# A state-space mixer: input tables from factors transposed once, tables by three products and two sums, stores from ScalarE's queue

## The chip, the cores and the metric

The kernel runs on one core of one Trainium2 chip. The metric is the device time of one execution, in microseconds (us); the figure given for a kernel is the median over its runs. The core has TensorE for matmuls and transposes (PE; its weight loads are shown apart as PEld), VectorE (DVE), ScalarE (ACT), GpSimd (POOL) and SyncE (SP), which here does nothing but issue transfers. A queue of transfers is served in the order in which its engine issues them, and an issue that waits for something holds back all that stand behind it.

## The reference

The program is a trunk of two layers on an input x of 1 x 1024 x 1024 in float32. Layer 0 projects the normalised input once, to an input u of a state-space mixer, to the queries, keys and values of a retention mixer, and to two gates; the two results are gated, put side by side and projected back. Layer 1 is a convolution module. The change touches only the state-space mixer of layer 0, which has 64 groups of 16 channels and 64 complex states each:

```python
    dt = jnp.exp(log_dt.astype(f32))[:, None]
    mag = jnp.exp(are * dt)
    lb_re = mag * jnp.cos(aim * dt)
    lb_im = mag * jnp.sin(aim * dt)
...
    bb_re = coef_re[..., None] * bre - coef_im[..., None] * bim
    bb_im = coef_re[..., None] * bim + coef_im[..., None] * bre
...
        bu_re = jnp.einsum('tbgh,gnh->tbgn', u_c, bb_re)
        bu_im = jnp.einsum('tbgh,gnh->tbgn', u_c, bb_im)
        pr, pim, zr, zi = lax.associative_scan(
            _complex_affine_combine, (a_r, a_i, bu_re, bu_im), axis=0)
        xr = zr + pr * s_re - pim * s_im
        xi = zi + pr * s_im + pim * s_re
        y = (jnp.einsum('tbgn,ghn->tbgh', xr, cre)
             - jnp.einsum('tbgn,ghn->tbgh', xi, cim)
             + dsk * u_c)
```

## The kernel before

**Stages.** The large products of layer 0's front are 128-column blocks of the input projection: u0 to u7, then the gates as blocks 8 to 23, then keys and values. Each block is two halves of 512 tokens, and each half is 8 x 3 matmuls of 128x512 (`mm3`, L276 to L278): operands are split into a high and a low part, and high by high, high by low and low by high are summed. u leaves for `u_d` in DRAM, the gates for `gs_d` and `gr_d`.

**The state-space part** runs beside the gates, one block of 8 groups (B = 0 to 7) for every two gate blocks. 1024 tokens are cut into 128 pieces of 8. For each B:

- `s5_tables(B)`: GpSimd makes three pairs of tables as outer products, through `outer`, six instructions a pair: Mr and Mi (powers of lambda 0 to 7 times the input coefficients bb; L790 to L792), the rotations Tc and Ts, and the output table W3 (powers 1 to 8 times C). ScalarE makes R8. These 18 instructions follow each other in a fixed chain over all blocks.
- `s5_states(B)`: U is loaded (L830). TensorE transposes Mr and Mi, four 128x128 pieces each (`w2r`, `w2i`, L837), ScalarE copies them to W2 (L839), and `v` = W2 by U (L848, 16 products). VectorE rotates, scans and rotates back on the bank of `v`, which gives the states S (L856 and following). Then `kp` (L882, L883; 8 products): the response within a piece of 8 tokens, from block-diagonal tables of C (`s_s_cbr`, `s_s_cbi`, loaded ready-made, 1 MB together) by Mr and Mi. ScalarE copies it to Kg (L885), VectorE adds the skip term `dd` to 16 columns, TensorE transposes it (`kt`, L888), ScalarE copies it to Kt (L890), it is stored to `k_d` (L892), and loaded back in Toeplitz form as Wd (L895), which ScalarE reorders into W1 (L897).
- `s5_out(B-1)`: `y` (24 products, L912 and L918) from W1 by U and W3 by S; ScalarE copies it to yb, which is stored to `y_d`.

Beside this the gate stage carries side work of other stages, each with its loads and stores: sums of the input, and on VectorE sums of the output projection's weights (`weight_sums`, `a` and `ws`).

**Before the first block**, `s5_params` makes the coefficients on VectorE, in a long chain of small instructions beside the u blocks; its last ones, bbr and bbi (L607, out of `s5bb`), are GpSimd's. Then the first tables follow (L785 to L792).

**What sets the order.** A scheduler places the instructions of each engine by a simulated timeline, within data dependences, numbers of buffers, `chained` (one instruction after another of its engine) and `issue_after` (not placed ahead of the named instruction). All transfers of this part are issued from SP's queue, as are all weight loads (`wf`). Pools `sums` and `s5w` open when the pool `ev` of the early tiles closes.

Of the kernel before, what the change touches and what calls it, by code (L numbers as in the profile page):

```python
# [57 lines left out]
class Trunk:  # L58
# [278 lines left out]
    def layer0_front(self, st):  # L337
# [100 lines left out]
        def u_block(nb):  # L438
            ut = uv.tile([P, 8, P], F32, name=f"ut_{nb}", tag="ut", bufs=2)

            def evac(h, ps):
# [3 lines left out]
                    r.rearrange("p (m j) -> p j m", j=8), op=ALU.mult)  # L445
            if nb < 2:
                for h in range(2):
                    evac(h, u01[nb][h])
# [4 lines left out]
        def gate_block(nb, w, dst):
# [8 lines left out]
            nc.sync.dma_start(dst[k * P:(k + 1) * P], gt[:])  # L462
# [18 lines left out]
        for nb in range(8, 24):
            B = (nb - 8) // 2
            if nb % 2 == 0:
                self.s5_states(B)
# [101 lines left out]
    def s5_params(self, sp, tp):  # L586
# [35 lines left out]
        v.tensor_scalar(self.cbni[:], self.cbni[:], -1.0, None, op0=ALU.mult)  # L622
# [162 lines left out]
    def outer(self, B, o_r, o_i, ar, ai, br, bi, view, op_r=ALU.subtract, op_i=ALU.add):  # L785

        gp = self.nc.gpsimd
        for o, op, (a0, b0), (a1, b1) in ((o_r, op_r, (ar, br), (ai, bi)), (o_i, op_i, (ar, bi), (ai, br))):
# [1 line left out]
            yield gp.tensor_tensor(view(t[:]), a1, b1, op=ALU.mult)  # L790
            yield gp.tensor_tensor(view(o), a0, b0, op=ALU.mult)
            yield gp.tensor_tensor(o, o, t[:], op=op)  # L792

    def s5_tables(self, B):
# [977 lines left out]
```

## Time and profile before

| | |
|---|---|
| median of 3 runs | 1176.35 us (1176.0 to 1176.86) |
| profiled execution: span | 1173.9 us, 2.45 under the median |
| TensorE busy (PE) | 1161.3 us, 99% |
| VectorE busy | 910.5 us, 78% |
| ScalarE busy | 545.1 us, 46% |
| GpSimd busy | 713.5 us, 61% |
| DMA | 270.66 MB, mean 231 GB/s |

The profile is of one execution. Its span runs from the first to the last instruction, and the medians hold something more around it. Busy time is the time in which an instruction runs on an engine, without waits, branches and transfer issues. A row of a group gives the line, the engine, the operation, the outputs and inputs by the program's names, shapes and the count; a row of a timeline begins with the start, in us from the span's start, and the duration. A matmul's duration is from its start to its modelled end, and overlaps with the next one's, so prices of TensorE's work are taken from distances between starts. The state-space blocks stand between about 100 and 345 us of the span.

### The profile page before, as it was taken

The numbers are of one execution on the slowest core, as the hardware profiler recorded it, in microseconds if no ns is written. First come the engines' busy times: TensorE is split into PE (matmuls) and PEld (weight loads), VectorE is DVE, ScalarE is ACT, GpSimd is POOL, SyncE is SP. The second block draws the span as 40 slices with busy tenths as digits, with TensorE's granted clock in tenths as the row PEclk, the third lists the DMA queues.
The fourth block names the chain that finished last, engine by engine and source line by source line (L and its number), as shares of the span: only waits on it lengthen the run. The fifth ranks groups of instructions, "written<-read, shape, count | busy, mean of one in ns | idle before, by whom it ended". The sixth has DMA issues, their size and how long they took to land.

```text
span 1173.9 us, 17492 instructions
## 1 busy us (share of the span) xinstructions
PE 1161.3 (99%) x6150; PEld 965.5 (82%) x6150; DVE 910.5 (78%) x1507; ACT 545.1 (46%) x821; POOL 713.5 (61%) x507
## 2 busy tenths in 40 slices
PE   9999999999999999999999999999999999999997
PEld 7888888888888888887788888888888888888887
DVE  7875789999717475689777888479999999999643
ACT  7212343332226642123645544367756678544662
POOL 2049999888843245664444034348894689977742
PEclk9999999999999999999999999999999999999999
DMA  9353378778789765765988468965448553357863
GB/s 344 109 178 109 134 270 312 272 269 282 273 307 325 268 228 192 251 190 180 362 313 304 160 220 268 309 232 188 161 158 306 216 182 132 134 176 243 281 247 138
DMA packets 131192, 270.66 MB, mean 231 GB/s; under 512 B 12832, under 2 KB 41760, under 8 KB 130976
## 3 DMA queue, kind: packets, MB, share of 16 engines
q1 hardware_dynamic: 129952, 265.35, 66.5%
q10 hardware_dynamic: 1152, 4.19, 0.9%
q8 instruction: 48, 0.79, 0.3%
q14 instruction: 40, 0.33, 0.1%
HBM read 193.54 MB, written 71.76 MB: 226 GB/s over the span
## 4 chain that ended last, share of the span: by engine, by line
PE 91%; DMA 4%; DVE 2%; SPq 1%; ACT 1%; POOL 1%; issue 1%; DVEq 0%; POOLq 0%; ACTq 0%
PE mm_g L277 8%; PE mm_g L278 8%; PE mm_g L276 7%; PE mm_w L278 4%; PE mm_w L277 4%; PE mm_w L276 4%; PE mm_a L278 2%; PE mm_b L277 2%; PE mm_a L276 2%; PE mm_b L278 2%; PE mm_a L277 2%; PE mm_b L276 2%; PE mm_u L278 2%; PE mm_oc L278 2%; PE mm_u L277 2%; PE mm_oc L277 2%
## 5 line engine op out<-in xcount | busy, mean ns | idle before, releaser
L1461 DVE SCALAR_TENSOR_TENSOR cv<-u,convw,cv 128x512 f32<-128x512 f32 x358 | 244.7, 750 | 5.0 <-ACT cv L1447 3.5
L1441 POOL TENSOR_TENSOR tp<-tp,tp 128x512 f32<-128x512 f32 x104 | 138.9, 1338 | 28.7 <-ACT tp L1440 23.4
L278 PE MATMUL mm_g<-xh,wl_g 128*128 128x512 f32 x256 | 100.8, 394 | 0.0
L277 PE MATMUL mm_g<-xl,wh_g 128*128 128x512 f32 x256 | 100.7, 394 | 0.0
L276 PE MATMUL mm_g<-xh,wh_g 128*128 128x512 f32 x256 | 100.5, 393 | 0.0
L1440 ACT ACTIVATE tp<-u,convw 128x512 f32<-128x512 f32 x104 | 69.6, 713 | 9.6 <-POOL tp L1441 9.4
L277 PEld LDWEIGHTS mm_g<-xl,wh_g 128*128 128x128 f32 x256 | 48.1, 188 | 11.2 <-issue 1.6
L278 PEld LDWEIGHTS mm_g<-xh,wl_g 128*128 128x128 f32 x256 | 48.0, 188 | 10.5
L276 PEld LDWEIGHTS mm_g<-xh,wh_g 128*128 128x128 f32 x256 | 48.1, 188 | 9.6
L278 PE MATMUL mm_oc<-zh,wl_woc 128*128 128x512 f32 (+1 forms) x152 | 54.5, 360 | 0.2 <-DMA wl_woc<-lo_woc 0.2
L276 PE MATMUL mm_oc<-zh,wh_woc 128*128 128x512 f32 (+1 forms) x152 | 54.3, 362 | 0.0
L277 PE MATMUL mm_oc<-zl,wh_woc 128*128 128x512 f32 (+1 forms) x152 | 54.0, 357 | 0.0
L276 PE MATMUL mm_glu<-yh,wh_glu 128*128 128x512 f32 x128 | 50.0, 392 | 1.3 <-ACT sg L1250 1.3
L277 PE MATMUL mm_u<-xl,wh_u 128*128 128x512 f32 x128 | 50.1, 391 | 1.0 <-DVE xl L390 0.9
L276 PE MATMUL mm_g<-h1h,wh_cg 128*128 128x512 f32 x128 | 50.3, 393 | 0.0
L276 PE MATMUL mm_a<-h1h,wh_ca 128*128 128x512 f32 x128 | 50.3, 393 | 0.0
L278 PE MATMUL mm_b<-h1h,wl_cb 128*128 128x512 f32 x128 | 50.3, 393 | 0.0
L232 ACT CAST lh<-lf 128x512 fp32r<-128x512 f32 x32 | 19.5, 618 | 65.9 <-DMA lf<-w_c 59.3
L278 PE MATMUL mm_a<-h1h,wl_ca 128*128 128x512 f32 x128 | 50.0, 391 | 0.0
L277 PE MATMUL mm_glu<-yl,wh_glu 128*128 128x512 f32 x128 | 50.0, 392 | 0.0
L278 PE MATMUL mm_g<-h1h,wl_cg 128*128 128x512 f32 x128 | 49.9, 390 | 0.0
L277 PE MATMUL mm_g<-h1l,wh_cg 128*128 128x512 f32 x128 | 49.9, 390 | 0.0
(811 smaller groups left out, 3637.3 us busy)
## 6 DMA issues: line engine op xcount, KB each, us to landing
wf_g<-w_ab SPq DMA_DIRECT2D x16, 512.0 KB, 5.4
a<-w_out SPq DMA_DIRECT2D x32, 256.0 KB, 4.4
ws<-a SPq DMA_DIRECT2D x32, 256.0 KB, 4.8
lf<-w_c SPq DMA_DIRECT2D x32, 256.0 KB, 5.3
wf_p<-ws SPq DMA_DIRECT2D x16, 512.0 KB, 4.1
wf_cb<-w_c SPq DMA_DIRECT2D x16, 512.0 KB, 4.9
wf_ca<-w_c SPq DMA_DIRECT2D x16, 512.0 KB, 4.7
wl_cb<-lo_cb SPq DMA_DIRECT2D x16, 512.0 KB, 3.4
```

The lines of the kernel that those rows point to most:

```text
L232: self.nc.scalar.copy(hi[:], f[:])
L276: nc.tensor.matmul(ps, wh[:, kb, :], xh, start=start, stop=False)
L277: nc.tensor.matmul(ps, wh[:, kb, :], xl, start=False, stop=False)
L278: self.last_mm = nc.tensor.matmul(ps, wl[:, kb, :], xh, start=False, stop=stop)
L1440: nc.scalar.mul(sk[:], u[:, k:k + HALF], cw[:, nb, k:k + 1])
L1441: gp.tensor_tensor(s0[:], s0[:], sk[:], op=ALU.add)
L1461: v.scalar_tensor_tensor(dst[:], *tap, accs_[i][:], op0=ALU.mult, op1=ALU.add)
```

## The change

Five things are done.

1. *Input tables from transposed factors.* After the first half of u6, `s5_turned` transposes the powers of lambda and bb once (12 transposes in three groups, three copies, four stores to DRAM). For each block four transposed factors are loaded, 256 KB each, repeated over partitions (PT and BT), and GpSimd multiplies them to W2 directly, six instructions without broadcast views. The transposes w2 and their copies go. U's load moves from `s5_states` into `s5_tables`.
2. *Three products and two sums.* Tc, Ts and W3 are made by `outer3`, five instructions a pair, from sums and differences of the factors that are made once.
3. *kp from the output table.* W3 grows to nine powers, and kp is a block-diagonal table of bb (filled by ScalarE) by W3. The skip term is added by four products of 16 columns with slices of the identity. kp comes out the other way round, so kt, its copy and VectorE's addition go, and Kg is stored in eight parts, with runs of 64 bytes.
4. *Queues.* The stores of the gates, of y and of k go from ScalarE's queue.
5. *Pools.* `ev` stays open through u6; the tiles of two temporary pools get fewer buffers. `input_sums_made` follows the last state instruction in place of the addition to Kg.

```diff
@@ layer0_front
             def evac(h, ps):
...
+                if (nb, h) == (6, 0):
+                    with tc.issue_after(self.last_mm.ins):
+                        self.s5_turned(ev)
...
-            nc.sync.dma_start(dst[k * P:(k + 1) * P], gt[:])
+            nc.scalar.dma_start(dst[k * P:(k + 1) * P], gt[:])
...
         u_block(4)
+        for nb in (5, 6):
+            u_block(nb)
         early.close()
         sums = self.pool("sums", 1, stack=st)
         self.s5 = self.pool("s5w", 1, stack=st)
-        for nb in range(5, 8):
-            u_block(nb)
+        u_block(7)
...
-                    with self.tc.issue_after(self.last_kg.ins):
+                    with self.tc.issue_after(self.last_s.ins):
                         self.input_sums_made(*odd)
@@ s5_params
-        self.cbr, self.cbni = load("s5_cbr", (NP, 32)), load("s5_cbi", (NP, 32))
+        self.bblk = [sp.tile([P, NP, 32], F32, name=f"s5_bblk{c}") for c in "ri"]
+        for b in self.bblk:
+            nc.gpsimd.memset(b[:], 0.0)
...
-        v.tensor_scalar(self.cbni[:], self.cbni[:], -1.0, None, op0=ALU.mult)
...
+        tt(self.psum[:], pr_[:], pi_[:], ALU.add)
...
+        tt(self.e2s[:], e2r[:], e2i[:], ALU.add)
+        tt(self.e1s[:], e1r[:], e1i[:], ALU.add)
+        self.last_phase = tt(e1i[:], e1i[:], e1r[:], ALU.subtract)
...
+        tt(self.cdif[:], self.cr[:], self.nci[:], ALU.add, gp)
+        tt(self.csum[:], self.cr[:], self.nci[:], ALU.subtract, gp)
...
-        tt(self.bbi[:], x1[2], x1[3], ALU.add, gp)
+        tt(self.bbr[:].rearrange("p h q -> p q h"), x1[0], x1[1], ALU.subtract, gp)
+        tt(self.bbi[:].rearrange("p h q -> p q h"), x1[2], x1[3], ALU.add, gp)
+
+    def s5_turned(self, tp):
+        nc = self.nc
+        self.pt_d = [self.dram.tile([8, 32, P], F32, name=f"pt{c}") for c in "ri"]
+        self.bt_d = [self.dram.tile([16, 32, P], F32, name=f"bt{c}") for c in "ri"]
+
+        def turn(name, srcs, dsts):
+            ps = self.bank(f"turn_{name}")
+            for i, src in enumerate(srcs):
+                nc.tensor.transpose(ps[:, i * P:(i + 1) * P], src, self.ident[:])
+            t = tp.tile([P, 8, P], F32, name=f"turned_{name}", tag="xin", bufs=8)[:, :4, :]
+            nc.scalar.copy(t.rearrange("p i n -> p (i n)"), ps[:])
+            n = len(srcs) // len(dsts)
+            for i, dst in enumerate(dsts):
+                nc.sync.dma_start(dst.rearrange("(i p) n -> p i n", p=P), t[:, i * n:(i + 1) * n, :])
...
+        turn("p", cols(self.pr[:, 0:8, :], 2) + cols(self.pi[:, 0:8, :], 2), [rows(d) for d in self.pt_d])
+        for c, b in zip("ri", (self.bbr, self.bbi)):
+            turn(f"b{c}", cols(b[:], 4), [rows(self.bt_d["ri".index(c)])])
+        for blk, b in zip(self.bblk, (self.bbr, self.bbi)):
+            for g in range(2):
+                r = slice(64 * g, 64 * g + 64)
+                nc.scalar.copy(blk[r, :, 16 * g:16 * g + 16], b[r].rearrange("p h q -> p q h"))
...
+    def outer3(self, B, o_r, o_i, k1, k2, k3, view, op_i):
+        gp = self.nc.gpsimd
+        t = self.big(f"o_{B}", "tmpP", 1)
+        yield gp.tensor_tensor(view(t[:]), *k1, op=ALU.mult)
+        yield gp.tensor_tensor(view(o_r), *k3, op=ALU.mult)
+        yield gp.tensor_tensor(o_r, t[:], o_r, op=ALU.subtract)
+        yield gp.tensor_tensor(view(o_i), *k2, op=ALU.mult)
+        yield gp.tensor_tensor(o_i, o_i, t[:], op=op_i)
+
     def s5_tables(self, B):
...
-        Mr, Mi = self.big(f"Mr_{B}", "Mr", 1), self.big(f"Mi_{B}", "Mi", 1)
...
-        made = [self.outer(B, Mr[:], Mi[:], bj(self.bbr), bj(self.bbi), pj(self.pr), pj(self.pi), vm)]
...
+        made = [self.outer3(B, Tc[:], Ts[:], (ea(self.e2s), eb(self.e1[0])), (ea(self.e2[0]), eb(self.e1[1])),
+                            (ea(self.e2[1]), eb(self.e1s)), vt, ALU.add)]
+        PT, BT = ([self.big(f"{n}{c}_{B}", n + c, 1) for c in "ri"] for n in ("PT", "BT"))
+        for t, d in zip(PT, self.pt_d):
+            nc.sync.dma_start(t[:], bass.AP(tensor=d.tensor, offset=d.offset + qs.start * P,
+                                            ap=[[32 * P, 8], [0, 16], [1, 4 * P]]))
+        for t, d in zip(BT, self.bt_d):
+            nc.sync.dma_start(t[:], bass.AP(tensor=d.tensor, offset=d.offset + qs.start * P,
+                                            ap=[[0, 8], [32 * P, 16], [1, 4 * P]]))
+        W2 = [self.big(f"W2{c}_{B}", f"W2{c}", 1) for c in "ri"]
+        made.append(self.outer(B, W2[0][:], W2[1][:], BT[0][:], BT[1][:], PT[0][:], PT[1][:], lambda ap: ap))
+
+        W3 = w.tile([P, 2, 4, 9 * 16], F32, name=f"W3_{B}", tag="W3", bufs=2)
+        for c, t in enumerate((self.cr, self.nci)):
+            nc.scalar.copy(W3[:, c, :, 0:16], t[:, qs, :])
+        made.append(self.outer3(B, W3[:, 0, :, 16:], W3[:, 1, :, 16:], (pj(self.psum), bj(self.cr)),
+                                (pj(self.pr), bj(self.cdif)), (pj(self.pi), bj(self.csum)), vm, ALU.subtract))
         self.s5_last = self.chained(chain(*made), self.s5_last)
-        R8 = self.big(f"R8_{B}", "R8", 2)
+        U = w.tile([P, 8, P], F32, name=f"U_{B}", tag="U", bufs=2)
+        nc.sync.dma_start(U[:], self.u_d[B].rearrange("j h g m -> (j h) g m"))
+        R8 = self.big(f"R8_{B}", "R8", 1)
@@ s5_states
-        U = w.tile([P, 8, P], F32, name=f"U_{B}", tag="U", bufs=2)
-        nc.sync.dma_start(U[:], self.u_d[B].rearrange("j h g m -> (j h) g m"))
-        W2 = []
-        for nm, M in (("r", Mr), ("i", Mi)):
-            ps = self.bank(f"w2{nm}_{B}")
-            for q in range(4):
-                nc.tensor.transpose(ps[:, q * P:(q + 1) * P], M[:, q, :], self.ident[:])
-            t = self.big(f"W2{nm}_{B}", f"W2{nm}", 1)
-            nc.scalar.copy(t[:].rearrange("p q n -> p (q n)"), ps[:])
-            W2.append(t)
...
-        kp = self.bank(f"kp_{B}")
-        for q in range(4):
-            o = kp[q * 32:(q + 1) * 32, :P]
-            nc.tensor.matmul(o, self.cbr[:, q0 + q, :], Mr[:, q, :], start=True, stop=False)
-            nc.tensor.matmul(o, self.cbni[:, q0 + q, :], Mi[:, q, :], start=False, stop=True)
+        kp, made = self.bank(f"kp_{B}"), []
+        rows = [slice(q * 32, (q + 1) * 32) for q in range(4)]
+        made += [nc.tensor.matmul(kp[r, :P], self.bblk[0][:, q0 + q, :], W3[:, 0, q, :P], start=True, stop=False)
+                 for q, r in enumerate(rows)]
+        made += [nc.tensor.matmul(kp[r, :16], self.ident[:, r], self.dd[:, B, :], start=False, stop=False) for r in rows]
+        made += [nc.tensor.matmul(kp[r, :P], self.bblk[1][:, q0 + q, :], W3[:, 1, q, :P], start=False, stop=True)
+                 for q, r in enumerate(rows)]
+        self.chained(made)
         Kg = w.tile([P, P], F32, name=f"Kg_{B}", tag="Kg", bufs=1)
         nc.scalar.copy(Kg[:], kp[:, :P])
-        self.last_kg = v.tensor_tensor(Kg[:, :16], Kg[:, :16], self.dd[:, B, :], op=ALU.add)
-        kp = self.bank(f"kt_{B}")
-        nc.tensor.transpose(kp[:, :P], Kg[:], self.ident[:])
-        Kt = w.tile([P, P], F32, name=f"Kt_{B}", tag="Kg", bufs=1)
-        nc.scalar.copy(Kt[:], kp[:, :P])
-        nc.sync.dma_start(self.k_d[B, 112:], Kt[:])
+        kd = self.k_d[B, 112:].rearrange("(j i) (g o) -> g i j o", j=8, g=8)
+        for g in range(8):
+            nc.scalar.dma_start(kd[g], Kg[16 * g:16 * g + 16].rearrange("p (j o) -> p j o", j=8))
@@ s5_out
-        nc.sync.dma_start(self.y_d[B].rearrange("i h g m -> (i h) g m"), yb[:])
+        nc.scalar.dma_start(self.y_d[B].rearrange("i h g m -> (i h) g m"), yb[:])
```

The order of TensorE around one state block (the fourth), before: `mm_g` are the gate's large matmuls, `w2r` and `w2i` the transposes of the tables.

```order
L278 MATMUL mm_g13_1_1844<-xh_7_1_218,wl_g13_1513 128x512
L837 MATMUL w2r_3_1928<-ident_69,Mr_3_1872 128x128 x4
L837 MATMUL w2i_3_1935<-ident_69,Mi_3_1873 128x128 x4
L276 MATMUL mm_g14_0_2008<-xh_0_0_134,wh_g14_1701 128x512
...
L276 MATMUL mm_g14_0_2008<-xh_7_0_214,wh_g14_1701 128x512
L848 MATMUL v0_3_1942<-U_3_1926,W2r_3_1933 64x128 x8
L848 MATMUL v1_3_1951<-U_3_1926,W2i_3_1940 64x128 x8
L882 MATMUL kp_3_1980<-Mr_3_1872,s5_s5_cbr_474 32x128
L883 MATMUL kp_3_1980<-Mi_3_1873,s5_s5_cbi_476 32x128
...
L277 MATMUL mm_g15_0_2116<-xl_0_0_135,wh_g15_1811 128x512
L888 MATMUL kt_3_1992<-ident_69,Kg_3_1989 128x128
L912 MATMUL y0_2_2064<-U_2_1615,W1_2_1688 128x128
```

The eight transposes stand 22 large matmuls ahead of v, and kt stands 28 large matmuls behind kp, just ahead of y. The same place on TensorE after, from the end of gate block 13 (`s5_bblkr` and `s5_bblki` are the block-diagonal tables, `s5_s5_dd` the skip term):

```order
L278 MATMUL mm_g13_1_1881<-xh_7_1_218,wl_g13_1552 128x512
L902 MATMUL v0_3_1971<-U_3_1944,W2r_3_1919 64x128 x8
L902 MATMUL v1_3_1980<-U_3_1944,W2i_3_1920 64x128 x8
L935 MATMUL kp_3_2009<-W3_3_1921,s5_bblkr_474 32x128 x4
L937 MATMUL kp_3_2009<-s5_s5_dd_478,ident_69 32x16 x4
L938 MATMUL kp_3_2009<-W3_3_1921,s5_bblki_475 32x128 x4
L276 MATMUL mm_g14_0_2043<-xh_0_0_134,wh_g14_1738 128x512
```

The transposes ahead of the gate block and kt within it are gone; v and kp stand together between two gate blocks, kp with four products more, and y stands alone, a whole gate block (48 large matmuls) later.

TensorE at the start, after: the transposes of `s5_turned` (`s5_pr`, `s5_pi`: powers, `s5_bbr`, `s5_bbi`: coefficients) among the `mm_u`, and block 0.

```order
L806 MATMUL turn_p_957<-ident_69,s5_pr_574 128x128 x2
L806 MATMUL turn_p_957<-ident_69,s5_pi_575 128x128 x2
L806 MATMUL turn_br_966<-ident_69,s5_bbr_728 128x128 x4
L806 MATMUL turn_bi_974<-ident_69,s5_bbi_729 128x128 x4
...
L902 MATMUL v0_0_1122<-U_0_1115,W2r_0_1090 64x128 x8
...
L902 MATMUL v1_0_1131<-U_0_1115,W2i_0_1091 64x128 x8
...
L935 MATMUL kp_0_1160<-W3_0_1092,s5_bblkr_474 32x128 x4
L937 MATMUL kp_0_1160<-s5_s5_dd_478,ident_69 32x16 x4
...
L938 MATMUL kp_0_1160<-W3_0_1092,s5_bblki_475 32x128 x4
```

The 12 transposes stand after the first half of u6, 72 `mm_u` ahead of the first gate block. In blocks 0 and 1 the halves of v (block 0) and of kp are parted by large matmuls (block 0: 10 `mm_g`, v, 6 `mm_g`, v, 17 `mm_g`, kp, 2 `mm_g`, kp; in block 1 kp is parted from v by 13 and cut by 4).

SP's queue in a block after the change, with the semaphores for which an issue waits in brackets (DMAHW: an earlier transfer; PE, DVE, Pool, Activation: an engine):

```order
L866 DMA PTi_5_2506<-pti_954 128x1x512 [waits DMAHW5_49,Pool_49]
L869 DMA BTr_5_2507<-btr_955 128x1x512 [waits DMAHW6_49]
L869 DMA BTi_5_2508<-bti_956 128x1x512 [waits DMAHW7_49]
L244 DMA a3_2_2254<-w_out 128x512 [waits DMAHW0_49]
L948 DMA Wd_3_2032<-k_d_84 128x8x128 [waits DMAHW3_49,DMAHW1_49]
L244 DMA a0_2_2248<-w_out 128x512 [waits DMAHW2_49]
L254 DMA ws7_0_1959<-a1_1_2130 128x512 [waits DVE_49]
L881 DMA U_4_2241<-u_d_82 128x1024 [waits DMAHW5_49,PE_49]
L265 DMA wf_g20_2630<-w_ab 128x1024 [waits DMAHW6_49,DVE_49]
L254 DMA ws6_0_1960<-a2_1_2132 128x512 [waits DMAHW7_49,DVE_49]
L254 DMA ws3_0_1961<-a3_1_2134 128x512 [waits DMAHW0_49,DVE_49]
```

The stores of k, y and the gates no longer stand in this queue; U stands behind the four table loads, behind Wd and behind a store of weight sums.

More of the change, by code (lines that the diff above doesn't have):

```diff
@@ L718, in s5_params @@
         self.pr, self.pi = pr_, pi_
+        self.psum = t((9, NP), keep="s5_psum")
+        tt(self.psum[:], pr_[:], pi_[:], ALU.add)
+        self.cdif, self.csum = t((NP, 16), keep="s5_cdif"), t((NP, 16), keep="s5_csum")
         self.r8 = t(keep="s5_r8")
@@ L769, in s5_params @@
             tt(cfi[:], a1[:], rden[:], ALU.mult)
-        self.bbr, self.bbi = t((NP, 16), keep="s5_bbr"), t((NP, 16), keep="s5_bbi")
+        self.bbr, self.bbi = (tp.tile([P, 16, NP], F32, name=f"s5_bb{c}") for c in "ri")
         bc = lambda q: q[:].unsqueeze(2).broadcast_to([P, NP, 16])
@@ L778, in s5_params @@
         tt(x1[3], br[:], bc(cfi), ALU.mult, gp)
-        tt(self.bbr[:], x1[0], x1[1], ALU.subtract, gp)
-        tt(self.bbi[:], x1[2], x1[3], ALU.add, gp)
+        tt(self.bbr[:].rearrange("p h q -> p q h"), x1[0], x1[1], ALU.subtract, gp)
[13 more added lines that the diff above has]
+                nc.sync.dma_start(dst.rearrange("(i p) n -> p i n", p=P), t[:, i * n:(i + 1) * n, :])
+        fl = lambda t: t.rearrange("p a b -> p (a b)")
+        cols = lambda t, n: [fl(t)[:, i * P:(i + 1) * P] for i in range(n)]
+        rows = lambda d: d[:].rearrange("a b n -> (a b) n")
+        turn("p", cols(self.pr[:, 0:8, :], 2) + cols(self.pi[:, 0:8, :], 2), [rows(d) for d in self.pt_d])
[5 more added lines that the diff above has]
+                nc.scalar.copy(blk[r, :, 16 * g:16 * g + 16], b[r].rearrange("p h q -> p q h"))
@@ L854, in s5_states @@
         vr, vi = V[0][:], V[1][:]
-        t2, t4 = (fl(self.big(f"m{i}_{B}", "tmpV", 4)) for i in range(2))
+        t2, t4 = (fl(self.big(f"m{i}_{B}", "tmpV", 2)) for i in range(2))
         v.tensor_tensor(t2, vi, ts, op=ALU.mult)
@@ L868, in s5_states @@
         zr, zi = (z.rearrange("p (q n) -> p q n", q=4) for z in (vr, vi))
-        t2, t3 = (self.big(f"d{i}_{B}", "tmpV", 4) for i in range(2))
+        t2, t3 = (self.big(f"d{i}_{B}", "tmpV", 2) for i in range(2))
         v.tensor_tensor(c0(t2), c0(zi), c0(Ts), op=ALU.mult)
@@ L917, in products @@
                         r = slice(64 * g2, 64 * g2 + 64)
-                        yield nc.tensor.matmul(ps[g2][:, cols(q)], W3[r, c, q, :], S[r, c, q, :],
+                        yield nc.tensor.matmul(ps[g2][:, cols(q)], W3[r, c, q, 16:], S[r, c, q, :],
                                                start=False, stop=q == 3 and c == 1)
```

26 lines of the change are left out of this document (9 added, 17 removed).

## The prediction

> **What bounds the kernel now.** I read the page's busy table first, then the chain of waits, then what TensorE itself waited for.
>
> ```profile
> span 1173.9 us, 17492 instructions
> PE 1161.3 (99%) x6150; PEld 965.5 (82%) x6150; DVE 910.5 (78%) x1507; ACT 545.1 (46%) x821; POOL 713.5 (61%) x507
> PEclk9999999999999999999999999999999999999999
> PE 91%; DMA 4%; DVE 2%; SPq 1%; ACT 1%; POOL 1%; issue 1%; DVEq 0%; POOLq 0%; ACTq 0%
> PE mm_glu L276 <- ACT sg L1250: 1.3, 1, 1.3
> PE rt L1182 <- DVE on L1174: 1.0, 1, 1.0
> ```
>
> TensorE is busy 99% of the span at the full granted clock and holds 91% of the chain that ended last; no wait of it inside the body is over 1.3 us. So a microsecond of TensorE work taken out of the state-space stage is a microsecond off the end, as long as no new wait appears in it. Next I cut the stage into its state blocks, one for two gate blocks.
>
> ```profile
> 131.00:160.50 29.50, 29.50 (x203) 24.69 (x202) 24.90 (x30) 10.37 (x19) 27.68 (x21) 1.00 0.62 226
> 190.00:219.50 29.50, 29.50 (x202) 24.70 (x201) 28.10 (x32) 9.54 (x18) 27.33 (x20) 1.00 0.85 292
> ```
>
> The columns are the stretch, its length, PE, PEld, DVE, ACT and POOL busy, the granted clock, the DMA share and GB/s. A block takes 29.5 us. TensorE is full, VectorE reaches 28.1 and GpSimd 27.7: three engines are nearly full, and a lighter TensorE is worth something only down to the next of them.
>
> **What is removed.** The price of a TensorE group is what it shifts the large matmuls around it, from the timeline of the first block.
>
> ```profile
> 100.67 0.39 PE L278 MATMUL mm_u<-xh,wl_u 128*128 128x512 f32 x1
> 100.90 0.60 PE L837 MATMUL w2r<-ident,Mr 128*128 128x128 f32 x4
> 101.34 0.60 PE L837 MATMUL w2i<-ident,Mi 128*128 128x128 f32 x4
> 101.69 0.48 PE L276 MATMUL mm_g<-xh,wh_g 128*128 128x512 f32 x1
> 102.70 0.39 PE L277 MATMUL mm_g<-xl,wh_g 128*128 128x512 f32 x1
> 106.58 0.39 PE L276 MATMUL mm_g<-xh,wh_g 128*128 128x512 f32 x1
> 106.90 1.09 PE L848 MATMUL v<-U,W2r 128*64 128x128 f32 x16
> 108.80 0.45 PE L882 MATMUL kp<-Mr,s_s_cbr 128*32 128x128 f32 x8
> 109.39 0.50 PE L277 MATMUL mm_g<-xl,wh_g 128*128 128x512 f32 x1
> 109.73 0.39 PE L278 MATMUL mm_g<-xh,wl_g 128*128 128x512 f32 x1
> 115.65 0.39 PE L277 MATMUL mm_g<-xl,wh_g 128*128 128x512 f32 x1
> 115.88 0.27 PE L888 MATMUL kt<-ident,Kg 128*128 128x128 f32 x1
> 116.68 0.40 PE L278 MATMUL mm_g<-xh,wl_g 128*128 128x512 f32 x1
> ```
>
> A large matmul starts every 0.227 us (109.73 to 115.65 is 26 of them, 5.92 us). From 100.67 to 102.70 there are five, worth 1.14 of the 2.03 us: the eight transposes w2r and w2i cost 0.90. From 115.65 to 116.68 there are four, worth 0.91 of 1.03: the transpose kt costs 0.12. Both go in all eight blocks: 8 x 1.02 = 8.2 us.
>
> **What is added on TensorE.** First, four products of 16 columns per block, which put the skip term into kp. Each f32 product here is two instructions (kp: 8 products, 16 instructions), so eight instructions more. No row shows 16 columns. The nearest is kp itself: 109.39 - 108.80 = 0.59 us for 16 instructions with 32 weight columns, 0.037 each, so 0.30 per block and 2.4 in all; that is the value I take. From below they cost nothing, if the small ones slip between the others; from above each pays its own weight load alone:
>
> ```profile
> L882 PEld LDWEIGHTS kp<-Mr,s_s_cbr x64: 105/108/110, 108.8 to 311.4; 128*32 128x32 f32 x64
> ```
>
> that is 8 x 0.108 = 0.86 per block, 6.9 in all.
>
> The Trainium skill ("TensorE: Matmul & The Clock Gate", LDWEIGHTS) has a weight load last as long as its columns over 1.2 in ns, whatever its rows: 27 ns for 32 columns. The rows here go the same way (0.110 us a transpose, 0.037 a kp instruction); by the page the addition would be an estimated 0.21 per block, and the sum 0.7 us better.
>
> Second, twelve transposes once, in three groups of four like w2r (101.34 - 100.90 = 0.44): 1.3 us. Third, in blocks 0 and 1 the program order cuts v and kp apart with large matmuls between, five more changes of kind. Going in costs 106.90 - 106.58 - 0.23 = 0.09 and coming out 109.73 - 109.39 - 0.23 = 0.11, so 0.20 each and 1.0 in all (from below nothing, since kt alone with its two changes cost 0.12). Added: 2.4 + 1.3 + 1.0 = 4.7. TensorE's balance is -3.5 us, between -6.9 (cheap ends) and +1.0 (dear ends).
>
> **GpSimd's tables.** They fall from 18 to 16 instructions per block.
>
> ```profile
> 81.64 1.29 POOL L607 TENSOR_TENSOR s_bbi<-s5bb 128x512 f32<-128x512 f32 x1
> 83.01 1.11 POOL L790 TENSOR_TENSOR o<-s_bbi,s_pi 128x512 f32<-128x512 f32 x1
> 92.36 2.40 POOL L791 TENSOR_TENSOR Tc<-s_e2r,s_e1r 128x512 f32<-128x512 f32 x1
> 223.65 1.11 POOL L791 TENSOR_TENSOR Mr<-s_bbr,s_pr 128x512 f32<-128x512 f32 x1 [3.21 <-PE kp L883]
> ```
>
> The six that make W2 read plain tiles (like s_bbi, 1.29) in place of broadcast ones (1.11), so nothing is won by them in time; two fewer at 1.1 to 2.4 us leave some 23 us of work in a block of 28.7. It already had 3.21 us to spare per block. The gain here is zero, hidden under TensorE. VectorE loses kp's small addition; ScalarE loses three copies. VectorE's 28.1 less that addition is still under 28.7, so it sets nothing, but its cover is thin: if its rows lengthen by a microsecond per block, the gain is gone in the four fullest blocks.
>
> **The new wait: the first table.** W2 of block 0 now waits for a round trip: s_bbi, transposes, ScalarE's copies, stores, loads, six GpSimd instructions.
>
> ```profile
> 38.80 0.69 DVE L622 TENSOR_SCALAR s_s_cbi<-s_s_cbi 128x1024 f32<-128x1024 f32 x1
> 66.61 0.43 DVE L607 TENSOR_TENSOR s5t<-s_e1r 128x256 f32<-128x256 f32 x1
> 84.08 1.03 ACT L267 CAST wh_g<-wf_g 128x1024 fp32r<-128x1024 f32 x1
> 102.36 0.59 ACT L839 COPY W2i<-w2i 128x512 f32<-128x512 f32 x1
> a<-w_out SPq DMA_DIRECT2D x32, 256.0 KB, 4.4
> u_d<-ut SPq DMA_DIRECT2D x8, 512.0 KB, 3.5
> DMA to landing us min/median/max: 3.2/3.8/7.7
> ```
>
> VectorE gets three sums of 288, 544 and 544 columns ahead of the coefficients (256 cost 0.34 apart, so 1.8) and loses the 0.6 of s_s_cbi: s_bbi ends at 82.9 + 1.0 = 83.9. TensorE reaches the transposes 72 large matmuls before 100.90, at 84.6, so they wait for nothing. ScalarE then has two copies into the block tiles, the cast of wh_g and three turned copies: 83.9 + 1.0 + 1.0 + 1.5 = 87.4. Four stores issue by 88.8 and land by 92.3 (3.5), the loads behind them by 97.4 (0.4 + 4.4, and a little for their queueing). GpSimd: W2 at 6 x 1.29 is done at 105.1, W3 at 111.0, the next T at 117.8, W2 of block 1 at 125.5, its W3 at 131.4. TensorE: the last mm_u ends at 102.2, the imaginary half of v comes at 106.9, the second half of kp at 112.9, v of block 1 at 128.1, its kp at 133.1. The margins are 1.8, 1.9, 2.6 and 1.7 us. Each microsecond that the loads land after 99 is one on TensorE. The stores can be 4 us later (7.7) and the loads some 3: at most 5 us of stall, at least none. I take 0.5.
>
> **The queues.** ScalarE's own stores cost it issue time: gates 2, y 1, kp 8 per block.
>
> ```profile
> 364.72 0.34 ACTq L934 DMA_DIRECT2D yn_d<-yn  x1
> 191.52 1.90 PE v L848 x32
> 203.65 0.42 SPq L830 DMA_DIRECT2D U<-u_d  x1
> U<-u_d SPq DMA_DIRECT2D x8, 512.0 KB, 4.6
> Wd<-k_d SPq DMA_DIRECT2D x8, 512.0 KB, 5.1
> 328.37 0.38 SPq L892 DMA_DIRECT2D k_d<-Kt  x1
> 318.93 0.26 ACT L890 COPY Kt<-kt 128x128 f32<-128x128 f32 x1
> ```
>
> Eleven at 0.34 are 3.7 us on an engine that was busy 9.5 of 29.5: no cost. The four table loads, 1 MB per block, raise 292 GB/s by 1.05 MB in 28.7 us, 37, to some 329 in the fullest block, and by the same ratio the DMA share from 0.85 to 0.96: nearly full, but no cost while nothing urgent stands behind them. U is what is late next. It was issued 12.1 us after v (203.65 against 191.52), because y stood there; now y comes a whole gate block after kp, so U can go at 3.0 + 10.9 + 1.8 = 15.7 after v and lands at 20.3, with 28.7 to go: 8.4 us of margin. I take no cost.
>
> **The sum.** -3.5 + 0.5 = -3.0: the span goes from 1173.9 to 1170.9. The profiled execution's span is 2.45 us under the median of the three runs, 1176.35; with the same 2.45 around it the time is 1173.3.
>
> **The rivals.** *The round trip is late and gives the gain back.* For it: seven steps on five queues with 1.7 us of margin, in a stretch where ScalarE and the load queue also carry the gate weights. Against it: the loads' median rows. It decides from a landing at 100.2; with the 5 us bound the time is 1173.3 + 4.5 = 1177.8, so 1174.0 to 1178. *The 16-column products are dear.* At the weight-load bound 4.5 us more: 1177.8. For it, only that nothing here shows such a product; against it, the overlap in kp.
>
> *Slower: U comes too late in every block.* On SP, U stands behind Wd, which waits for the eight kp stores, and behind a weight-sum store that waits for VectorE. Kg is copied 3.4 us after v, the stores are issued by 6.4; with landing L and a hold H of SP, U is issued at 7.2 + L + H, and v waits once this passes 28.7 - 4.6 = 24.1, that is L + H over 16.9. For it: the DMA share of 0.96, and that SP held k_d back by 9.2 us in the last block (319.19 to 328.37), and the stores are 1024 pieces of 64 bytes per block, where the 1024 pieces of 512 of u_d took 3.5, 7.7 at worst. L = 7.7 and H = 9.2 just reach it; with U also at 7.7 it is 3.1 late. Against it: every hold would have to fall in every block. One microsecond late in each of seven blocks is 1180.3, 3.1 is 1195.
>
> The Trainium skill ("DMA: Bandwidth & Descriptors", Specifications) speaks for this rival: under 512 B a transfer is done as read-modify-write. If that doubled L from 3.5 to an estimated 7, L + H would be 16.2, still short. No row of the profile has such pieces.
>
> *The change doesn't do what it says*: GpSimd's instructions drop by 16, and nothing follows, since GpSimd had slack; that is inside the forecast.
>
> **How the numbers follow.** A measurement of this kernel tells about 0.2% (2.35 us) from no change. Forecast, more than that won: 0.53. Round trip late: 0.24, dear products: 0.06, both within 0.2%. U late: 0.17, slower. Predicted 1173.3. The low end is TensorE's cheap end with no stall, 1176.35 - 6.9 = 1169.5, less 0.5 for the reading of the rows: 1169.0. The high end holds both middle rivals and the mildest form of the slower one, 1180.0, and leaves out the rest of it. Faster 0.53, same 0.30, slower 0.17.
>
> **What would show it.** Right: the block from v to v near 28.8 us; kp near 0.9; no w2 or kt rows; GpSimd waiting several us per block; no TensorE wait above 1 us before 140 us. Wrong: a PE wait for GpSimd's W2 or W3 in blocks 0 and 1 (the round trip), for the landing of U (the slower rival), or VectorE filling its blocks.

## The result, and the profile after

The changed kernel takes 1208.4 us (median of 4 runs, 1206.86 to 1209.47) against 1176.6 for the kernel before: the ratio is 1.026, with a 95% interval of 1.0243 to 1.0277. It is slower by 31.8 us, and 35 above the forecast. The page of its profile, and what TensorE waited for (us in total, times, longest):

```profile
span 1205.0 us, 17613 instructions
PE 1165.4 (97%) x6154; PEld 965.3 (80%) x6154; DVE 910.7 (76%) x1502; ACT 542.7 (45%) x820; POOL 702.2 (58%) x495
PE 76%; DMA 11%; DVE 5%; POOL 4%; issue 2%; ACT 1%; SPq 1%; ACTq 0%; DVEq 0%; POOLq 0%
...
PE v L902 <- DMA U<-u_d: 17.3, 4, 7.0
PE v L902 <- POOL W2r L834: 6.6, 1, 6.6
```

Before, TensorE waited nowhere for more than 1.3 us and held 91% of the chain of waits. Now transfers hold 11% of the chain, and v waits once for the first tables and four times for U: two of the rivals happened together. TensorE's timeline shows where, and a second loss behind each wait (rows of v, kp and the first large matmul behind kp; in brackets the wait):

```profile
112.11 1.98 PE L902 MATMUL v<-U,W2r 128*64 128x128 f32 x16 [6.58 <-POOL W2r L834]
...
168.28 1.09 PE L902 MATMUL v<-U,W2r 128*64 128x128 f32 x16
...
170.17 0.43 PE L935 MATMUL kp<-W,s_bblkr 128*32 128x128 f32 x8
...
170.81 0.50 PE L276 MATMUL mm_g<-xh,wh_g 128*128 128x512 f32 x1
...
200.54 1.09 PE L902 MATMUL v<-U,W2r 128*64 128x128 f32 x16 [3.69 <-DMA U<-u_d]
...
237.69 1.97 PE L902 MATMUL v<-U,W2r 128*64 128x128 f32 x16 [7.04 <-DMA U<-u_d]
...
242.42 0.69 PE L276 MATMUL mm_g<-xh,wh_g 128*128 128x512 f32 x1
...
268.94 1.09 PE L902 MATMUL v<-U,W2r 128*64 128x128 f32 x16 [0.28 <-DMA U<-u_d]
...
303.80 1.97 PE L902 MATMUL v<-U,W2r 128*64 128x128 f32 x16 [6.24 <-DMA U<-u_d]
...
334.13 1.09 PE L902 MATMUL v<-U,W2r 128*64 128x128 f32 x16
```

Undisturbed, v and kp take 170.81 - 168.28 = 2.53 us; behind the wait of 7 us they take 242.42 - 237.69 = 4.73. The whole second loss is read from one v to the next. An undisturbed block takes 28.50 us (shown with the last experiments). Less the wait at its end, the block behind the wait of 3.69 takes 30.1 us, the one behind 7.04 takes 31.0 and the one behind 6.24 takes 30.3: 1.6, 2.5 and 1.8 us more. In the first block the halves of v start 4.64 us apart (112.11 and 116.75), and 2.61 in a run without that wait (105.89 and 108.50): 2.0 more. The stretches around the wait of 7 us say why (columns as in the prediction; the granted clock stands ahead of the DMA share):

```profile
233.50:237.50 4.00, 0.00 (x0) 0.00 (x0) 1.21 (x2) 2.41 (x5) 1.97 (x2) 0.50 1.00 374
237.50:239.00 1.50, 1.31 (x13) 1.34 (x15) 0.00 (x0) 1.46 (x2) 0.00 (x0) 0.50 1.03 385
243.00:245.00 2.00, 2.00 (x10) 1.64 (x9) 2.00 (x4) 0.00 (x0) 1.92 (x3) 1.00 1.09 329
```

The granted clock falls to half while TensorE waits and stays there for some 5 us of work here, and for 3.4 to 4.4 behind the three other waits. In the wait itself the transfer engines are full: 374 GB/s, a share of 1.00.

The span is longer by 1205.0 - 1173.9 = 31.1 us. How much of it arises in the state-space stage is read at the first key matmul (`mm_k`), and a later point is the first `kv`. Their rows, before and then after (the number ahead of "to" is the first start):

```profile
L276 PE MATMUL mm_k<-xh,wh_k x64: 388/389/477, 333.0 to 515.4; 128*128 128x512 f32 x64
...
L1107 PE MATMUL kv<-v,kt x112: 272/273/324, 447.5 to 555.4; 128*64 128x128 f32 x112
```

```profile
L276 PE MATMUL mm_k<-xh,wh_k x64: 389/389/477, 362.5 to 547.3; 128*128 128x512 f32 x64
...
L1160 PE MATMUL kv<-v,kt x112: 272/273/323, 479.8 to 587.1; 128*64 128x128 f32 x112
```

The key matmul is 29.5 us later than before. That is made of 7.9 us of waits for the first two blocks' tables (6.58 and three small ones), 17.3 for U, 7.9 of half clock behind them (2.0 + 1.6 + 2.5 + 1.8), and 0.7 by which TensorE's first product of the span starts later (6.73 in place of 6.00). These are 33.8; the rest, -4.3, is TensorE's balance, forecast at -3.5. Another 2.8 us come up to the first `kv`, 1.3 of them a wait for `kraw`, to which the store of the last y leads below. Behind it 1.2 are won back, for which no run looked for a cause.

### The profile page after: what moved, and what is told of

It reads as the page before. It is cut to its first block, busy times and chain, and to the rows that moved or that the text cites. A ratio compares the mean times of both kernels' runs of the same rounds, so it can differ in the third digit from the quotient of the medians.

```text
span 1205.0 us, 17613 instructions
## 1 busy us (share of the span) xinstructions
PE 1165.4 (97%) x6154; PEld 965.3 (80%) x6154; DVE 910.7 (76%) x1502; ACT 542.7 (45%) x820; POOL 702.2 (58%) x495
## 4 chain that ended last, share of the span: by engine, by line
PE 76%; DMA 11%; DVE 5%; POOL 4%; issue 2%; ACT 1%; SPq 1%; ACTq 0%; DVEq 0%; POOLq 0%
PE mm_w L276 4%; PE mm_w L277 4%; PE mm_w L278 4%; PE mm_g L276 4%; PE mm_g L278 4%; PE mm_g L277 4%; PE mm_a L278 2%; PE mm_a L276 2%; PE mm_b L277 2%; PE mm_a L277 2%; PE mm_b L276 2%; PE mm_b L278 2%; PE mm_oc L278 2%; PE mm_oc L277 2%; PE mm_oc L276 2%
## 5 line engine op out<-in xcount | busy, mean ns | idle before, releaser
L276 PE MATMUL mm_u<-xh,wh_u 128*128 128x512 f32 x128 | 49.6, 398 | 1.1 <-ACT wh_u L267 0.9
L268 DVE TENSOR_TENSOR wl_g<-wf_g,wh_g 128x1024 fp32r<-128x1024 f32 x16 | 26.5, 1655 | 31.6 <-ACT wh_g L267 31.6
L166 ACT CAST wh_p<-wf_p 128x1024 fp32r<-128x1024 f32 x28 | 29.4, 1052 | 46.4 <-PE mm_w L277 38.5
```

The source lines that it names most:

```text
L166: self.nc.scalar.copy(wh[:].rearrange(fl), wf[:])
L268: lo[i].tensor_tensor(wl[:].rearrange(fl)[:, c], wf[:, c], h.bitcast(F32), op=ALU.subtract)
L276: nc.tensor.matmul(ps, wh[:, kb, :], xh, start=start, stop=False)
```

## The experiments

Each ratio is to runs of the kernel before that were taken beside it, whose medians lie between 1177.0 and 1178.6 us.

### The first tables: the fills on ScalarE

ScalarE and SP ahead of the first block, of the changed kernel, and the longest transfer of that stretch in its chain of waits (start, us, what):

```profile
84.76 2.40 ACT L822 COPY s_bblkr<-s_bbr 64x512 f32<-64x512 f32 x2 [14.61 <-POOL s_bbr L611]
87.17 2.33 ACT L822 COPY s_bblki<-s_bbi 64x512 f32<-64x512 f32 x2
...
91.44 0.60 ACT L808 COPY turned_bi<-turn_bi 128x512 f32<-128x512 f32 x1
```

```profile
93.01 0.39 SPq L811 DMA_DIRECT2D ptr<-turned_p  x1
...
94.66 0.64 SPq L811 DMA_DIRECT2D bti<-turned_bi  x1
...
99.50 0.58 SPq L869 DMA_DIRECT2D BTi<-bti  x1
```

```profile
99.50 8.57 DMA BTi<-bti
```

The scheduler put the four fills of the block-diagonal tables (4.7 us) ahead of the copies of the turned factors. The stores went at 93.0 to 95.3, and the last load landed at 99.50 + 8.57 = 108.1; the forecast had 88.8 and 97.4.

```diff
+        with self.tc.issue_after(self.last_turn.ins):   # the last copy of a turned group
             for blk, b in zip(self.bblk, (self.bbr, self.bbi)):
                 ... nc.scalar.copy(blk[r, ...], b[r]...)
```

> The changed kernel with one thing moved: ScalarE fills the block-diagonal tables behind the three copies of the turned factors instead of ahead of them. Theory (stalls): the changed kernel loses 6.6 + 1.3 us of waits for the first two blocks' tables and some 2.1 us more to the slower clock behind the first of them; the fills are 4.7 us of that chain, so the stores and the loads come some 4.5 us earlier, the wait of 6.6 falls to about 2, and 4.5 to 7 us are won: 1201.5 to 1204. Rival (the transfers of the round trip set it, the fills were hidden): within 1 us of the changed kernel's 1208.4.

Measured: 1202.1, ratio 1.0213 (1.0188 to 1.0238). The waits for the first tables fell from 7.9 to 2.5 us, the longest is 0.8, and no half clock follows them; 0.47% was won, about 5.5 us. The theory holds: the order on ScalarE was the larger part of this stall.

### U: is it Wd ahead of it, the queue, the bytes?

```diff
 # s5_states: the load of Wd and the copy W1 go; s5_out, ahead of y:
+        with self.tc.issue_after(self.last_u.ins):     # U of the next block
+            nc.sync.dma_start(Wd[:], ...)
+        nc.scalar.copy(W1[:]..., Wd[:]...)
```

> The changed kernel with the load of Wd and the copy to W1 written ahead of the block's y in place of behind kp, and Wd's load not placed ahead of the next block's U. Theory (U behind Wd behind the k stores): the four waits for U, 17.3 us, and the slower clock behind them, some 5 us, go: 1186 to 1189. Rival (the transfer engines are too full with 1 MB more per block, so that U lands late wherever it stands): waits for U remain, less than 6 us won, 1202 or more.

Measured: 1215.8, ratio 1.0343 (1.0309 to 1.0376): the theory missed, and the kernel is slower still. U went ahead of Wd and v still waited for it; now y waits too, for W1's copy on ScalarE:

```profile
PE y L967 <- ACT W L959: 11.9, 2, 6.1
PE v L902 <- DMA U<-u_d: 11.1, 3, 5.2
...
187.51 1.04 ACT L959 COPY W<-Wd 128x1024 f32<-128x1024 f32 x1 [9.43 <-DMA k_d<-Kg]
```

So Wd alone was not what made U late. The longer wait of y ends with the copy in the last row, which stood on ScalarE behind the eight k stores. With the late fills as well:

> Both edits of the two other runs together. Theory (the stalls are all of the loss, and behind them stands the 3 us gain on TensorE that was forecast): the first wait about 2 us, no wait for U: 1176 to 1181. Rival (something else than the two stalls costs time): 1185 or more.

Measured: 1208.9, ratio 1.0268 (1.025 to 1.0286): the theory missed again, with waits of 12.7 us for U and 9.7 of y for W1's copy. Next, every store back on SP's queue:

```diff
-            nc.scalar.dma_start(dst[k * P:(k + 1) * P], gt[:])      # and kd[g], y_d[B]
+            nc.sync.dma_start(dst[k * P:(k + 1) * P], gt[:])
```

> The changed kernel with the stores of the gates, of y and the eight of k issued from SP's queue again. Theory (the eight k stores, each of which waits for an earlier transfer's semaphore, hold whichever queue issues them, and Wd and then U stand behind them): U is as late as in the changed kernel, and SP's other loads later: 1205 to 1220. Rival (it is ScalarE's being held while it issues, late gates and late copies, that delays everything): the waits for U go and the time falls below 1195.

Measured: 1206.2, ratio 1.0246 (1.0228 to 1.0264), with 15.5 us of waits for U and one of v of 4.2 that ends with a cast on ScalarE. The queue of the stores was not the cause of this stall either. In the changed kernel, these rows show TensorE's y, whose reading frees the buffer of the U that came 7 us late, then what stands on SP ahead of that U, and its landing in the chain of waits:

```profile
215.62 1.95 PE L965 MATMUL y<-U,W 128*128 128x128 f32 x16
```

```profile
218.46 0.60 SPq L866 DMA_DIRECT2D PTr<-ptr  x1
...
220.62 0.68 SPq L866 DMA_DIRECT2D PTi<-pti  x1
222.71 0.58 SPq L869 DMA_DIRECT2D BTr<-btr  x1
223.34 0.58 SPq L869 DMA_DIRECT2D BTi<-bti  x1
...
224.58 0.38 SPq L948 DMA_DIRECT2D Wd<-k_d  x1
225.01 3.07 SPq L244 DMA_DIRECT2D a<-w_out  x1
228.13 1.73 SPq L254 DMA_DIRECT2D ws<-a  x1
229.95 0.38 SPq L881 DMA_DIRECT2D U<-u_d  x1
```

```profile
229.95 7.60 DMA U<-u_d
```

The buffer is free at 217.6, 17.0 after v (forecast 15.7). U is issued 12.4 us later, behind 1 MB of table loads, Wd and weight sums, and lands 7.6 us after its issue. Four runs tell the loads from the k stores, and the loads' bytes from their places in the queue.

```diff
-        for t, d in zip(PT, self.pt_d):
+        for t, d in zip(PT, self.pt_d) if B == 0 else ():       # the same for BT; tiles kept
```

> The changed kernel with the turned factors loaded for block 0 only; the later blocks multiply block 0's factors again (their results are not computed), so 7 MB of loads are left out. Theory A (the loads, which stand just ahead of U, fill the transfer engines and make U land in 8 to 10 us): U lands in 4 to 5 us, its waits fall from 17.3 to under 6 us, 1190 to 1196. Theory B (U is issued late because SP stands at Wd behind the eight k stores): the waits stay over 12 us, 1202 or more.

```diff
-        for g in range(8):
-            nc.scalar.dma_start(kd[g], Kg[16 * g:16 * g + 16].rearrange("p (j o) -> p j o", j=8))
+        nc.scalar.dma_start(self.k_d[B, 112:], Kg[:])
```

> The changed kernel with Kg stored as it stands by one transfer of 64 KB in place of eight with runs of 64 bytes (its columns then lie in the wrong order in memory). Theory B (eight stores hold ScalarE, Wd and U): the waits for U fall under 6 us, 1190 to 1196. Theory A (the table loads): the waits stay over 12 us, 1202 or more.

Both edits together:

> Both: factors loaded for block 0 only, and Kg by one transfer as it stands. If either cause alone makes U late, as much as the better of the two single runs; if it needs both, no wait for U is left and about 22 us are won, 1184 to 1188, with the waits for the first tables (some 8 us and the slower clock) still in it.

And the same issues with an eighth of the bytes:

```diff
+        n = 8 if B == 0 else 1
-            nc.sync.dma_start(t[:], bass.AP(..., ap=[[32 * P, 8], [0, 16], [1, 4 * P]]))
+            nc.sync.dma_start(t[:16 * n], bass.AP(..., ap=[[32 * P, n], [0, 16], [1, 4 * P]]))   # BT alike
```

> The changed kernel with the four loads of the turned factors kept in their place in the queue with their waits, but each filling only 16 of 128 partitions after block 0 (the other partitions keep block 0's factors, so the later blocks' tables are not computed): 7 of 8 MB are left out, the issues stay. Theory A1 (it is the bytes: the transfer engines are full when U is issued): as with the loads left out altogether, waits for U under 6 us, 1188 to 1194. Theory A2 (it is the issues, which wait for GpSimd to be done with the buffers and hold SP ahead of U): waits for U over 12 us, 1202 or more.

| run | us | ratio (interval) | waits for U |
|---|---|---|---|
| factors loaded once | 1190.4 | 1.0103 (1.0067 to 1.0139) | 3.4 |
| one k store | 1200.7 | 1.0197 (1.0171 to 1.0224) | 14.0 |
| both | 1189.8 | 1.0097 (1.0081 to 1.0114) | none |
| an eighth of the bytes, same issues | 1194.8 | 1.0147 (1.0132 to 1.0163) | 3.4 |

The waits of the first and the second, in that order; the fourth has the same row as the first:

```profile
PE v L905 <- DMA U<-u_d: 3.4, 1, 3.4
```

```profile
PE v L902 <- DMA U<-u_d: 14.0, 4, 6.9
```

The greater part is the bytes. With the same issues in the same places and an eighth of the bytes (and of the rows that they fill), U waits as little as without the loads. The eight stores of k give the last 3.4 us of waits; in time the runs with and without them do not differ (1.0103 and 1.0097). The wait of 7.0 has both causes: at that place v waits 6.9 us with one k store, 3.4 with an eighth of the bytes, and not at all with both causes out. That the issue of the eight is slow is seen on ScalarE's queue of the changed kernel, with the landing of the last of them out of the chain of waits:

```profile
211.75 8.69 ACTq L945 DMA_DIRECT2D k_d<-Kg  x8
```

```profile
219.97 3.43 DMA k_d<-Kg
```

Issuing the eight takes 8.7 us, in which ScalarE does nothing else. In the trace each of them waits for a semaphore, and four of these waits end when a transfer of the weight sums lands (three `a<-w_out`, one `ws<-a`). The last of the eight, 8 KB in runs of 64 bytes, itself lands in 3.4 us, about what the prediction took for L. (The read-modify-write that the Trainium skill, "DMA: Bandwidth & Descriptors", Specifications, has below 512 B has no price that can be seen here.)

### Can the whole computation be rescued?

The late fills stay, and U is loaded one block ahead:

```diff
+        U = w.tile([P, 8, P], F32, name=f"U_{B}", tag="U", bufs=3)     # ahead of the factors; W1: bufs=1
+        nc.sync.dma_start(U[:], self.u_d[B].rearrange("j h g m -> (j h) g m"))
         PT, BT = ...
```

> The changed kernel with the late fills, and with three buffers for U in place of two (and one for W1 in place of two, to make room), so that U of a block is loaded one block ahead of its use. Theory (the two stalls are the whole loss, and behind them stands the gain on TensorE): no wait for U, 0 to 2 us of waits for the first tables, 1174 to 1179. Rival (the eight k stores and 1 MB more per block cost time by other waits as well, as they did when Wd was moved): another wait of TensorE takes their place, 1184 or more.

Measured: 1196.5, ratio 1.0156 (1.014 to 1.0172). No wait for U is left, but others took its place: one of 3.4 us for GpSimd's rotations, and these, where ScalarE shows what they hang on:

```profile
PE v L903 <- ACT yb L976: 9.9, 3, 5.9
...
226.37 1.04 ACT L951 COPY W<-Wd 128x1024 f32<-128x1024 f32 x1 [9.79 <-DMA Wd<-k_d]
```

W1's copy waits 9.8 us for Wd, the copies of y stand behind it, and v's second half waits for a bank that they free. The stores of the gates and of y from SP besides (the edits shown above, together):

> The whole computation: the changed kernel with the late fills, U one block ahead (three buffers, W1 one) and all stores but k's from SP's queue. Theory (the table loads and the eight k stores remain, so Wd, W1 and the copies behind it on ScalarE stay late): 1186 to 1197. Rival (the queue of the stores was what made Wd late): 1180 or less.

Measured: 1191.6, ratio 1.0113 (1.0093 to 1.0133), the wait for yb 11.5. No version of the whole computation with the turned factors came under the kernel before.

### Is the gain on TensorE there, and what is left?

The late fills, the factors of block 0 only and the one k store, together:

> The changed kernel with the late fills, the factors loaded for block 0 only and Kg stored as it stands by one transfer: all three costs found so far are out (with the work named). Theory (behind the stalls stands the forecast gain on TensorE): no wait over 2 us in the state-space stage, from v to v 28.6 us, 1174 to 1180. Rival (TensorE's balance was no gain, or a wait elsewhere is left): 29.3 us or more from v to v without a wait, 1182 or more.

Measured: 1180.1, ratio 1.0023 (1.0011 to 1.0035). TensorE's timeline of this run, v of two neighbouring blocks, and the same of the kernel before:

```profile
160.22 1.09 PE L906 MATMUL v<-U,W2r 128*64 128x128 f32 x16
...
188.72 1.09 PE L906 MATMUL v<-U,W2r 128*64 128x128 f32 x16
```

```profile
161.94 1.09 PE L848 MATMUL v<-U,W2r 128*64 128x128 f32 x16
...
191.45 1.09 PE L848 MATMUL v<-U,W2r 128*64 128x128 f32 x16
```

A block takes 28.50 us in place of 29.51, so the gain on TensorE is real. Yet this run, which leaves out the later blocks' tables and the right order of k, was not under the kernel before. Parts 2 and 4 alone, in the kernel before, looked for the rest:

```diff
-        made.append(self.outer(B, Tc[:], Ts[:], ...))        # and W3
+        made.append(self.outer3(B, Tc[:], Ts[:], ...))
```

> The kernel before with part 2 of the change alone: Tc, Ts and W3 by three products and two sums (and the fewer buffers that make room for the sums of factors). Theory (GpSimd had slack): within 0.2% of the kernel before, 1174 to 1179. Rival (GpSimd's 27 of 29.5 us slow VectorE or hold the tables): faster than 1174.

Measured: 1177.1, ratio 0.9991 (0.9983 to 1.0000). GpSimd's busy time fell from 713.5 to 689.9 us and nothing followed, as forecast.

```diff
-            nc.sync.dma_start(dst[k * P:(k + 1) * P], gt[:])            # and k_d (Kt, one store), y_d
+            nc.scalar.dma_start(dst[k * P:(k + 1) * P], gt[:])
```

> The kernel before with part 4 of the change alone: the stores of the gates, of y and of k (one transfer of 64 KB per block here) from ScalarE's queue. Theory (the queue alone costs nothing, the eight stores and the loads do): within 0.2%, 1174 to 1179. Rival (ScalarE, held at its issues by transfers of the other queue, is late with copies that TensorE needs): 1181 or more.

Measured: 1183.6, ratio 1.0044 (1.0031 to 1.0057): the theory missed, and the queue alone costs about 5 us. In this run, ScalarE's queue and VectorE at the end of the state-space stage; then the kernel before, SP's queue and VectorE:

```profile
350.48 0.33 ACTq L924 DMA_DIRECT2D y_d<-yb  x1
...
359.63 1.29 DVE L987 TENSOR_TENSOR kraw<-mm_k,R 128x512 f32<-128x512 f32 x2 [11.90 <-DMA y_d<-yb]
```

```profile
348.98 0.33 SPq L924 DMA_DIRECT2D y_d<-yb  x1
...
352.81 1.29 DVE L987 TENSOR_TENSOR kraw<-mm_k,R 128x512 f32<-128x512 f32 x2 [6.62 <-DMA y_d<-yb]
```

The first step on the keys (kraw) takes over the memory of yb and waits for the last y to be stored. From SP that store is issued ahead of the rotary tables (1 MB) and the input's loads and lands in 3.8 us; from ScalarE's queue it goes 1.5 us later, behind them, and lands in 9.2. TensorE then waits 1.8 us for kraw and falls to the lower clock. This store alone:

```diff
-        nc.sync.dma_start(self.y_d[B]...)
+        (nc.scalar if B == 7 else nc.sync).dma_start(self.y_d[B]...)
```

> The kernel before with one transfer moved: the store of y of the last block (512 KB) from ScalarE's queue. Theory (this store lands some 9 us after its issue in place of 4, since the rotary tables' and the input's loads of SP then stand ahead of it, and VectorE's first step on the keys waits for its buffer): all of the cost of part 4 alone, 1181 to 1185. Rival (the cost of part 4 comes from the gates' stores or from ScalarE being held): within 0.2% of the kernel before.

Measured: 1180.4, ratio 1.0020 (1.0009 to 1.0031). Neither theory holds alone: it is about half of part 4's price. The traces show where the other half arises, as far as one profile of each run can: the first `kv` starts at 447.5 us before, at 449.7 with this store alone, and at 453.1 with all of part 4. Of the 3.4 us between the last two, 1.0 is a wait of v for W2r's copy, which stood on ScalarE behind a late load of the input, and 1.0 is a longer wait for `kraw` (1.77 in place of 0.75). Only behind the longer one does the clock fall to half, for 3.4 us, which loses an estimated 1.7. What made that load late was not tested.

And the run with the late fills, the factors of block 0 only and the one k store, with all stores from SP:

> As the run with the late fills, block 0's factors only and one plain store of Kg, and beside that the stores of the gates, of y and of k from SP's queue again. Theory (the last 7 us by which that run missed the forecast are the queue of the stores, above all the last y): 1172 to 1176, at or a little under the kernel before. Rival (TensorE's gain is lost later by something else): 1178 or more.

Measured: 1177.1 against 1178.6 for the kernel before on the same chip, ratio 0.9985 (0.9973 to 0.9996): about 1.8 us under it, where the forecast had 3.0, which the interval just holds. So the forecast's gain comes out, in sign and about in size, once the bytes of the factors, the eight k stores, the fills' place and the queue are taken away. All four are parts of the change.

## Why the prediction was wrong, point by point

- **The step that failed first** is "the four table loads ... no cost while nothing urgent stands behind them. U is what is late next". The ratio of shares was worked out (0.96, nearly full), and then U was priced at its median landing of 4.6 us from a trace without these loads. With them it landed in 7.6 at the longest wait, and was issued 29.4 us after v where 15.7 was forecast, and where the rival had 24.1 as its limit. v waited for U in four blocks, 17.3 us. The worst landing stood in the prediction's own row: its 7.7 was read as a store of `u_d`, but that row holds the loads of U as well, and the 7.7 is a U (issued at 176.82 in the trace before). The rival was given 0.17 and its result was right; its cause was so in part only: the bytes, which it had through the DMA share, were the greater part, and the k stores the smaller. In the block of the longest wait the last k store was issued 19.9 us after v, where the rival had 6.4, and landed in 3.4, as it had.
- **The round trip**: "two copies into the block tiles" at 1.0 us were four, of 4.7, and the loads' 4.4 were 8.6. The margin of 1.7 us had no room for either (and 82.9 + 1.8 - 0.6 is 84.1, not the 83.9 it started from). The rival was given 0.24 and bounded at 4.5; it cost 7.9 of waits and 2.0 of half clock.
- **A mechanism that stands in no sum**: the granted clock. Each long wait was priced at itself; each cost 1.6 to 2.5 us more. The Trainium skill ("TensorE: Matmul & The Clock Gate", Part 1: The HAM clock gate) has it: about 3.4 us without work bring half rate, and as long of work the full one. The rows above agree on the half rate (clock 0.50), but less waiting was enough here (last section), and the prediction did not weigh that rule.
- **The queues**: "eleven at 0.34 are 3.7 us ... no cost" priced the issues and not the landing. The last y's store lost its place ahead of 1 MB of loads; part 4 alone costs 0.44%. Nor is the issue price right: the eight k stores of a block took 3.8 to 10.7 us to issue in the changed kernel, where eight at 0.34 are 2.7.
- **TensorE's balance** came near, -4.3 by the account above against -3.5, and 1.0 us per block against 0.72; that the sum fits is in part luck, since two of its terms missed in opposite directions. The 16-column products were taken too dear: kp takes 24 instructions in 0.64 us (170.17 to 170.81) where 16 took 0.59, so 0.05 per block and not 0.30, 2.0 us less in all; the dear-products rival falls. The cuts in blocks 0 and 1 were taken too cheap, at 1.0 for both: eight times 1.0 less 1.3 for the twelve transposes would be -6.7, so they cost an estimated 2.4. Block 1 alone, in the run with all stores from SP, takes 30.94 us from v to v, of which 1.49 are waits: 0.95 more than 28.50.
- **GpSimd's tables at zero** was right (0.9991). **VectorE's thin cover** showed in the runs without the loads or with an eighth of them, where kp waits 0.6 to 1.9 us for S, twice in the first of them and once in each of the others.

## What to carry to other kernels

Transposes on TensorE cost 0.9 us per block here; feeding the same tables through memory took no time of TensorE and 1 MB per block on transfer engines that were at 0.85, and that was dearer. When transfers are added to a stage that is nearly full, price the most urgent load behind them at the landing time of a full stretch, not at its median. Price a wait of TensorE of some 2 us or more with 1.6 to 2.5 us of half clock on top, as measured here. When a store changes its queue, ask which loads now stand ahead of it and who waits for its buffer.

## What the runs showed of the hardware

The drop of the clock does not go by the length of the wait alone. A wait of 3.43 us (v's second half at 193.57 in the run with U ahead) had none behind it, and one of 1.88 us (kp at 222.13 in the run with the late fills, block 0's factors and the one k store) had. Two stretches of the first run and two of the second (the columns are as above, the granted clock ahead of the DMA share):

```profile
188.50:191.91 3.41, 1.64 (x19) 1.04 (x17) 3.38 (x6) 0.14 (x1) 3.33 (x3) 1.00 1.01 372
191.91:195.32 3.41, 1.75 (x41) 1.41 (x41) 3.34 (x3) 2.27 (x5) 3.25 (x3) 1.00 0.81 300
```

```profile
220.03:223.43 3.40, 1.52 (x32) 1.04 (x28) 3.40 (x6) 0.20 (x1) 3.32 (x3) 1.00 1.01 395
223.45:226.85 3.40, 3.40 (x10) 2.65 (x9) 2.96 (x4) 2.14 (x4) 3.24 (x3) 0.50 0.70 221
```

In every trace of this case the granted clock changes only at times that lie whole multiples of 3.41 us apart; in the changed kernel, ahead of the end of its span, it is at half for 6.83, 3.41, 10.24 and 6.83 us. With each trace cut at these times, every stretch at full clock in which TensorE idled for more than 1.95 of the 3.41 us was followed by one at half clock, none with less than 1.75 was, and between them both occur. The wait of 3.43 us was cut into 1.77 and 1.66 by such a time, and the one of 1.88 lay within one stretch. The Trainium skill ("TensorE: Matmul & The Clock Gate", Part 1: The HAM clock gate) says that the window runs freely, which fits both; an idle window, which it asks for, was not needed here.

The other surprise is that the store of the last y did not get past the loads of the other queue when it was issued from ScalarE's: 512 KB took 9.2 us to land behind them, and 3.8 when it stood ahead of them.
